# Gates below the smallest normal number set to zero, and an expert list of 96 blocks in place of 99

## The chip, the cores and the metric

The kernel runs on one core of a Trainium2 chip. The core has a matrix engine (TensorE, PE in the profile; its weight loads are PEld), three engines for elementwise work (VectorE or DVE, ScalarE or ACT, GpSimd or POOL), a queue engine (SyncE or SP), and 16 DMA engines that all queues share. The metric is the device time of one execution in microseconds; less is better.

## The reference

One layer of a diffusion backbone for 256 latent tokens with 256 context tokens: a modulated norm, one wide input projection, an mLSTM and a differential attention beside each other, their gated merge, and at the end a retrieval of single-neuron experts. Only the last part matters here:

```python
s = jnp.einsum('bthpd,hpnd->bthpn', q, sub_keys)
s1, i1 = lax.top_k(s[..., 0, :], P_TOPK)
s2, i2 = lax.top_k(s[..., 1, :], P_TOPK)
cand_s = (s1[..., :, None] + s2[..., None, :]).reshape(B, T, P_HEADS, P_TOPK * P_TOPK)
cand_i = (i1[..., :, None] * N_KEYS + i2[..., None, :]).reshape(B, T, P_HEADS, P_TOPK * P_TOPK)
top_s, pos = lax.top_k(cand_s, P_TOPK)
idx = jnp.take_along_axis(cand_i, pos, axis=-1)
g = jax.nn.softmax(top_s, axis=-1)
...
act = jax.nn.gelu(jnp.einsum('td,ted->te', hx, expert_u[ix]), approximate=False)
return jnp.einsum('te,ted->td', (gx * act).astype(h.dtype), expert_v[ix])
```

Each token has 8 heads, and each head picks 16 of 16,384 experts, with a softmax over the 16 scores as their gates. The scores lie far apart, so many gates are extremely small; the reference's arithmetic turns a result below the smallest normal number, 2^-126, into zero. An expert whose gate is zero for a token adds nothing to it.

## The kernel before

Everything is float32. Where full precision is wanted on TensorE, a tile is split into a rounded part `hi` (ScalarE) and the rest `lo` (VectorE), and three products of the parts are summed.

The 256 tokens form two tiles of 128, and each tile four groups of 32 tokens. The retrieval goes in these steps:

- **Choice and gates** (`retrieve`, run once for each tile). VectorE finds the 16 best of each head; L1176 to L1180 make the softmax: subtract the greatest, exponential on ScalarE, sum, reciprocal, product. The result `e`, 128 x 128, is transposed into `gT`.
- **Gate map** (`gate_map`). From the chosen indices and `gT`, one-hot matmuls build the full table of gates, experts by tokens, which goes to device memory; beside it `most` keeps, for each expert and each group of 32 tokens, the greatest gate.
- **Lists** (`lists`). A planner on VectorE, TensorE, ScalarE and GpSimd sorts the experts with a gate above zero (`use`, the test on `most`) into lists of blocks of 128 experts. There are eight lists for one group of 32 tokens (6 blocks each), one for each tile (7 each), one for both tiles (21), 16 for pairs of groups, one of each tile (1 block each): `CAPS`, 99 blocks in all. What finds no place in the lists before the last goes into the one for both tiles, and what finds none there is counted in `n_over`. Empty places of a block point at a fixed row with gates of zero: every block is gathered and multiplied whole, whatever it holds. At the end of the planner, one-hot tiles `N_BLOCKS` wide (L1408 to L1412, 32 rounds) and matmuls turn the places into the row numbers `idxV` and `idxG`.
- **First expert matrix.** Meanwhile TensorE multiplies all of `expert_u` with the tokens (`u_pair`), and the results, after the Gelu, go to the same table in device memory (`ag_dram`). The steps above are issued between these matmuls, a few at a time (`pump`, with the rate `pace`).
- **Second expert matrix.** For each block GpSimd issues two indirect gathers (L1501): 128 rows of `expert_v` (8 KB each) into `vraw`, and 128 rows of gates and activations into `ag`. VectorE multiplies gates and activations into weights. A block for one group of 32 needs, for each of its tiles, four matmuls of 128 x 32 weights (`v_groups`, four blocks beside each other on the array; each matmul has two records in the trace). A block of the lists for a tile or for both tiles (`v_block`) is split into two halves of `hi` and `lo` and needs 12 matmuls of 128 x 512 for each tile, which is 12 or 24. Two further blocks (`DENSE`) are taken whole.

The order of the second part is written out: 20 blocks of the first tile's groups (`SOON`) beside the end of `expert_u`, then `ITEMS`. These are two one-tile groups of four blocks, the two dense blocks, then a mixture made by `spread` (which puts the members of each list at equal distances): two more one-tile groups of four, four pair groups of four, the list for both tiles and the lists of the tiles; and three one-tile groups at the end. One letter an item (S a one-tile group of four, P a pair group of four, B a block for both tiles, T a block for one tile, D dense), `ITEMS` is

```
SSDDBTBTBPBTBSTBBTBPTBBTBTBBTPBTBBSTBTBPBTBTBSSS
```

which is 81 blocks. `fetch` (L1553) issues the gathers ahead of the work, in order; the gathers of GpSimd and the matmuls on these accumulators keep the order of the program. There are 12 buffers of rows, given out in pairs, two blocks a pair. `fetch` rounds block numbers to pairs:

```python
while staged[0] < end[0]:
    b = staged[0]
    if (b + 4 * (b >= L - 8)) // 2 * 2 - 11 >= FIRST_OF[n] or vex is None and b > 7:
        break
```

`L` is the number of blocks in `ITEMS`, `FIRST_OF[n]` the first block of item `n`. The last eight blocks, those of the last two items, are held back until four rows of other data (residual stream and norm weights, L1725 to L1729) have been given buffers. At the very end come, in program order: the third item from the end, which closes the first tile; the fetch for the item before the last; `residual` and `finish_tile` of the first tile; the item before the last; the fetch for the last item; the last item; the second tile's residual and output.

The loop at L1672 takes care of entries beyond the lists: it runs only if `n_over` is above zero, 126 turns, each with loads of 128 rows and their matmuls.

Of the kernel before, what the change touches and what calls it, by code (L numbers as in the profile page):

```python
# [26 lines left out]
OP = mybir.AluOpType  # L27
# [26 lines left out]

N_LIST = P - 2
EARLY = 104
CAPS = (6,) * 8 + (7, 7, 21) + (1,) * 16
BASE = tuple(sum(CAPS[:i]) for i in range(len(CAPS)))
BOTH, PAIR, DENSE = 10, 11, 27
TILES = [(g // 4,) for g in range(8)] + [(0,), (1,)] + [(0, 1)] * 17  # L60
# [6 lines left out]

N_BLOCKS = sum(CAPS)
NOWHERE = N_BLOCKS * P
# [3 lines left out]
def spread(*groups):  # L73
    return [x for _, _, x in sorted(((i + 0.5) / len(g), j, x) for j, g in enumerate(groups) for i, x in enumerate(g))]
# [4 lines left out]
SETS = [[[(4 * t + j, i) for j in range(4)] for i in range(6)] for t in range(2)]  # L79
SOON = SETS[0][:5]  # L80
PAIRS = [[(PAIR + 4 * d + g, 0) for g in range(4)] for d in range(4)]
ITEMS = SETS[1][:2] + [[(DENSE, i)] for i in range(N_LIST, P)] + spread(
    SETS[1][2:4], PAIRS, [[(BOTH, i)] for i in range(CAPS[BOTH])], [[(8 + n % 2, n // 2)] for n in range(14)]) + [
    SETS[0][5], SETS[1][4], SETS[1][5]]


def build(tc, a, dump=None):
    nc = tc.nc
# [6 lines left out]
    def turn(*args):  # L95
        tc.keep_in_program_order(nc.tensor.transpose(*args))
# [73 lines left out]
    def b3(t, n):  # L170
        return t.unsqueeze(2).to_broadcast([P, t.shape[1], n])
# [921 lines left out]
    for k in range(KT):  # L1093
# [4 lines left out]
                                       op0=OP.add, op1=OP.subtract)  # L1098
# [19 lines left out]
    def top16(src, vals, idx):  # L1118
        for r in range(2):
            v = vals[:, r * 8:(r + 1) * 8]  # L1120
            nc.vector.max(v, src)
            nc.vector.max_index(idx[:, r * 8:(r + 1) * 8], v, src)
            if r == 0:
                nc.vector.match_replace(src, v, src, NEG)
# [36 lines left out]
    def retrieve(t):  # L1161
        tif = tk.tile([P, 16, 16], F32, name="tif", tag="tif", bufs=1)
        nc.vector.tensor_copy(tif, ti[t])
        tv4 = tv[t].rearrange("p (h s) i -> p h s i", s=2)
        ti4 = tif.rearrange("p (h s) i -> p h s i", s=2)
        gv = tk.tile([P, HEADS, 16], F32, name="gv", tag="gv", bufs=1)
        gp = tk.tile([P, HEADS, 16], U32, name="gp", tag="gp", bufs=1)
        for h in range(HEADS):
            cs = tk.tile([P, 16, 16], F32, name="cs", tag="cs", bufs=2)
            nc.gpsimd.tensor_tensor(cs, b3(tv4[:, h, 0, :], 16),  # L1170
                                    tv4[:, h, 1, :].unsqueeze(1).to_broadcast([P, 16, 16]), op=OP.add)
            top16(cs.rearrange("p a b -> p (a b)"), gv[:, h, :], gp[:, h, :])
            yield
        e = tk.tile([P, HEADS, 16], F32, name="e", tag="e", bufs=1)
        z = tk.tile([P, HEADS], F32, name="zz", tag="zz", bufs=1)
        nc.vector.tensor_tensor(e, gv, gv[:, :, 0:1].to_broadcast([P, HEADS, 16]), op=OP.subtract)  # L1176
        nc.scalar.activation(e, e, AF.Exp)
        nc.vector.reduce_sum(z, e, axis=AX.X)
        nc.vector.reciprocal(z, z)
        nc.vector.tensor_tensor(e, e, b3(z, 16), op=OP.mult)  # L1180
        pos = tk.tile([P, 2, HEADS, 16], U32, name="pos", tag="pos", bufs=1)
        nc.vector.tensor_scalar(pos[:, 0], gp, 4, None, op0=OP.logical_shift_right)
        nc.vector.tensor_scalar(pos[:, 1], gp, 15, None, op0=OP.bitwise_and)
        posf = tk.tile([P, 2, HEADS, 16], F32, name="posf", tag="posf", bufs=1)
        nc.vector.tensor_copy(posf, pos)
        yield
        ii = []
        for s in range(2):
            r = tk.tile([P, HEADS, 16], F32, name="ix", tag=f"ix{s}", bufs=1)
            for h in range(HEADS):  # L1190
                if h % 4 == 0:
                    four = tk.tile([P, 4, 16, 16], F32, name="oh", tag="oh", bufs=1)
                oh = four[:, h % 4]
                nc.vector.tensor_tensor(oh, b3(posf[:, s, h, :], 16),
                                        iota[:, 0:16].unsqueeze(1).to_broadcast([P, 16, 16]), op=OP.is_equal)
                nc.gpsimd.tensor_tensor(oh, oh, ti4[:, h, s, :].unsqueeze(1).to_broadcast([P, 16, 16]),
                                        op=OP.mult)
                if h % 4 == 3:
                    yield
                    nc.vector.reduce_sum(r[:, h - 3:h + 1], four, axis=AX.X)  # L1200
                if h % 2:
                    yield
            ii.append(r)
        yield
        ps = psG.tile([P, 4, P], F32, name="g", tag="g")
        for i, src in enumerate((ii[0], ii[1], e)):
            turn(ps[:, i, :], src.rearrange("p h i -> p (h i)"), ident)
            nc.vector.tensor_copy(slots[i][:, t * P:(t + 1) * P], ps[:, i, :])
        yield
# [83 lines left out]
    def lists():  # L1293
# [46 lines left out]
        def fill(kind, size, bases):  # L1340
            n, w = kind.shape[1:]
            at = blocks_at[:, fills[0], 0:n]
            fills[0] += 1
            for c, base in enumerate(bases):
                nc.gpsimd.memset(at[:, c:c + 1], float(base * P - NOWHERE))
            pre, tot = (psG.tile([P, 4, P], F32, name="g", tag="g").rearrange("p a b -> p (a b)")[:, 0:n * w].rearrange(
                "p (c i) -> p c i", c=n) for _ in range(2))
            rank = ls.tile([P, 4, N_LIST], F32, name="rank", tag="rank", bufs=2)[:, 0:n, 0:w]
            pw = put[:, 0:n, 0:w]
            yield  # L1350
            yield
            mp_(pre, lhsT=from_on, rhs=kind, start=True, stop=True)
            mp_(tot, lhsT=one, rhs=kind, start=True, stop=True)
            yield
            for c in range(n):
                nc.vector.tensor_tensor_scan(rank[:, c], tot[:, c], zero[:, 0:w], 0.0, op0=OP.add, op1=OP.add)
            yield
            nc.vector.tensor_tensor(rank, rank, pre, op=OP.add)
            nc.vector.scalar_tensor_tensor(pw, rank, float(size * P), kind, op0=OP.is_lt, op1=OP.mult)
            nc.vector.reduce_sum(gone[:, 0:w], pw.rearrange("p c i -> p i c"), axis=AX.X)  # L1360
            nc.gpsimd.tensor_tensor(rank, rank, at.unsqueeze(2).to_broadcast([P, n, w]), op=OP.add)
            nc.gpsimd.tensor_tensor(rank, rank, pw, op=OP.mult)
            nc.gpsimd.tensor_tensor(places[:, 0:n, 0:w], places[:, 0:n, 0:w], rank, op=OP.add)
            yield
# [11 lines left out]
        for t in range(2):  # L1376
            four = single[:, 4 * t:4 * t + 4]
            for first, n, w in ((0, CAPS[0] - 1, EARLY), (CAPS[0] - 1, 1, N_LIST)):
                yield from fill(four[:, :, 0:w], n, [BASE[4 * t + c] + first for c in range(4)])
# [4 lines left out]
        nc.vector.tensor_tensor(k3[:, 0], k3[:, 0], k2[:, 1], op=OP.add)  # L1384
        yield from fill(k2, CAPS[8], [BASE[8 + c] for c in range(2)])
        nc.vector.tensor_tensor(k3[:, 0], k3[:, 0], gone, op=OP.subtract)
        yield
        yield from fill(k3, CAPS[BOTH], [BASE[BOTH]])
        over = ls.tile([P, N_LIST], F32, name="over")
# [60 lines left out]
    def plan():  # L1450
        nonlocal vst, gates
        yield from retrieve(0)
        for _ in weave(gate_map(0), retrieve(1)):
            yield
        tk.release()
        vst = tc.alloc_tile_pool(name="vst", bufs=1, side="right", reuse_waits="tile")
        yield from gate_map(1)
        while leaving:
            step(leaving)
            yield  # L1460
        pace[0] = 1.6
        yield from lists()
        gates = tc.alloc_tile_pool(name="ag", bufs=1, side="right", reuse_waits="tile")
        pace[0] = 1.3
        yield from soon()

    n = P - N_LIST + 1
# [346 lines left out]
```

## Time and profile before

| | |
|---|---|
| median of 3 runs | 2348.71 us (2344.53 to 2353.24) |
| the profiled execution | 2340.29 us, its span 2338.4 us |
| granted TensorE clock, mean | 0.981 |
| PE busy, 0 to 500 / to 1000 / to 1500 / to 2046 us | 476.6 / 489.3 / 475.5 / 513.3 us |
| PE busy, 2046 to 2338.4 us | 243.4 of 292.4 us |
| DMA share there, GB/s | 0.87, 344 |
| blocks gathered (rows of `expert_v`) | 99 |

The span is the time from the first to the last instruction of the profiled execution; its whole time is 1.9 us more. DMA share is the mean busy share of the 16 DMA engines. A group of instructions in the profile is given as line, engine, operation, out<-in by the program's names, count, busy time, mean duration of one, and the idle time of the engine before them with what ended it. Matmuls overlap their neighbours in the records, so a mean duration times a count is more than the time they take.

### The profile page before, as it was taken

How to read it: one execution, taken by the hardware profiler on the slowest of the kernel's cores; microseconds unless marked ns; L12 is line 12 of the kernel's file. 1: busy time of each engine (PE TensorE's matmuls, PEld its weight loads, DVE VectorE, ACT ScalarE, POOL GpSimd, SP SyncE). 2: the span in 40 equal slices, each digit the busy share in tenths (PEclk: the TensorE clock that was granted, in tenths of full speed). 3: DMA queues.
4: the chain of work that ended last, by engine and by line, in shares of the span. 5: the costliest groups of instructions: out<-in, count | busy, mean ns of one | idle time of the engine just before them, and what ended most of it. 6: DMA issues, size and time to landing. Idle time of an engine off the chain costs nothing.

```text
span 2338.4 us, 37404 instructions
## 1 busy us (share of the span) xinstructions
PE 2198.0 (94%) x14184; PEld 1880.2 (80%) x14184; DVE 1570.3 (67%) x2760; ACT 1057.4 (45%) x1723; POOL 935.0 (40%) x957
## 2 busy tenths in 40 slices
PE   6999999999999999998999999999999989999994
PEld 3669988999899999887987888888787776756661
DVE  3357973767876858746799766876799944454553
ACT  3232232244566744444444777995335433333431
POOL 2132210236534200002235755772456454566553
PEclk9999999999999999998999999999999999999997
DMA  9968964866456588755556457878665588899895
GB/s 380 351 212 304 332 228 134 316 206 192 144 150 203 169 280 283 272 191 176 172 174 209 160 183 222 229 213 238 197 194 172 184 330 321 330 414 387 333 395 190
DMA packets 235910, 570.98 MB, mean 244 GB/s; under 512 B 85154, under 2 KB 118739, under 8 KB 221264
## 3 DMA queue, kind: packets, MB, share of 16 engines
q1 hardware_dynamic: 153888, 339.34, 44.1%
q0 software_dynamic: 46992, 211.67, 25.1%
q10 hardware_dynamic: 34848, 17.57, 2.6%
q8 instruction: 111, 1.82, 0.3%
q14 instruction: 71, 0.58, 0.1%
HBM read 524.33 MB, written 38.93 MB: 241 GB/s over the span
## 4 chain that ended last, share of the span: by engine, by line
PE 69%; DVE 12%; DMA 6%; issue 5%; ACT 3%; POOL 2%; ACTq 0%; another core or an unknown queue 0%; SPq 0%; DVEq 0%; POOLq 0%
PE acc L289 24%; PE s L93 18%; PE acc L278 11%; PE v L93 9%; DVE lo L136 4%; DMA raw<-expert_u 3%; PE g L93 2%; ACT hi L133 2%; PE m L433 1%; DMA vraw<-expert_v,idxV 1%; PE m L278 1%; DMA raw<-w_mod 1%; DVE at L1409 1%; DVE act L1625 1%; PE m L382 1%
## 5 line engine op out<-in xcount | busy, mean ns | idle before, releaser
L133 ACT CAST hi<-raw 128x1024 fp32r<-128x1024 f32 x528 | 551.6, 1048 | 803.9 <-PE acc L289 256.7
L136 DVE TENSOR_TENSOR lo<-raw,hi 128x1024 fp32r<-128x1024 f32 x457 | 599.7, 1316 | 283.6 <-ACT hi L133 279.2
L93 PE MATMUL s<-h,hi 128*128 128x512 f32 x2048 | 743.3, 404 | 3.2 <-ACT hi L133 2.6
L93 PE MATMUL s<-h,lo 128*128 128x256 f32 x2048 | 581.3, 284 | 33.2 <-DVE lo L136 20.8
L93 PEld LDWEIGHTS s<-h,hi 128*128 128x128 f32 x2048 | 388.6, 190 | 96.0 <-ACT hi L133 6.3
L93 PEld LDWEIGHTS s<-h,lo 128*128 128x128 f32 x2048 | 390.7, 191 | 45.5 <-DVE lo L136 28.6
L289 PE MATMUL acc<-hL,hi 128*128 128x256 f32 x2048 | 421.7, 286 | 0.0
L289 PEld LDWEIGHTS acc<-hL,hi 128*128 128x128 f32 x2048 | 342.5, 193 | 1.5
L289 PE MATMUL acc<-hL,lo 128*128 128x256 f32 x1024 | 292.3, 286 | 4.6 <-DVE lo L136 4.6
L136 POOL TENSOR_TENSOR lo<-raw,hi 128x1024 fp32r<-128x1024 f32 x71 | 176.9, 2492 | 254.3 <-ACT hi L133 248.6
L289 PEld LDWEIGHTS acc<-hL,lo 128*128 128x128 f32 x1024 | 197.5, 193 | 6.2 <-DVE lo L136 5.5
L117 POOL DMA_DIRECT2D raw<-w_mod x128 | 68.2, 533 | 300.2 <-DVE raw L522 278.7
L522 DVE SCALAR_TENSOR_TENSOR raw<-raw,cr 128x1024 f32<-128x1024 f32 x128 | 154.7, 1219 | 32.4 <-DMA raw<-w_mod 17.6
L1241 POOL TENSOR_SCALAR o<-iota,i1T,gT 128x128 f32<-128x128 f32 x128 | 138.9, 1092 | 93.1 <-PE g L93 49.3
L1517 DVE TENSOR_TENSOR lo<-vraw,hi 128x1024 fp32r<-128x1024 f32 x74 | 90.3, 1228 | 100.5 <-ACT hi L1515 76.1
L1501 POOL DMA_INDIRECT vraw<-expert_v,idxV x99 | 106.6, 1077 | 97.7 <-PE v L93 38.1
L289 PE MATMUL acc<-hC,hi 128*128 128x256 f32 x512 | 134.0, 283 | 0.0
L1515 ACT CAST hi<-vraw 128x1024 fp32r<-128x1024 f32 x74 | 77.1, 1049 | 115.0 <-PE v L93 56.1
L93 PE MATMUL v<-hi,l 128*128 128x512 f32 x448 | 123.5, 394 | 4.0 <-issue 3.1
L1625 DVE TENSOR_REDUCE act<-s 128x256 f32<-128x512 f32 x126 | 86.2, 684 | 53.6 <-PE s L93 48.2
L1501 POOL DMA_INDIRECT ag<-ag_dram,idxG x99 | 106.3, 1074 | 33.6 <-issue 27.3
L93 PE MATMUL v<-vraw,w 128*32 128x512 f32 x640 | 90.2, 642 | 28.5 <-DVE w L1536 12.9
(427 smaller groups left out, 3859.9 us busy)
## 6 DMA issues: line engine op xcount, KB each, us to landing
raw<-expert_u SPq DMA_DIRECT2D x256, 512.0 KB
raw<-w_in SPq DMA_DIRECT2D x176, 512.0 KB
raw<-w_mod POOLq DMA_DIRECT2D x128, 512.0 KB
raw<-w_mod SPq DMA_DIRECT2D x64, 512.0 KB
raw<-w_out SPq DMA_DIRECT2D x32, 512.0 KB
raw<-w_pq SPq DMA_DIRECT2D x32, 512.0 KB
ag_dram<-gates SPq DMA_DIRECT2D x32, 512.0 KB
ag_dram<-act ACTq DMA_DIRECT2D x126, 128.0 KB
```

The lines of the kernel that those rows point to most:

```text
L93: tc.keep_in_program_order(mm(*args, **kw))
L117: d = queue.dma_start(r, src)
L133: nc.scalar.copy(h, r)
L136: (nc.vector if shared[0] else nc.gpsimd).tensor_tensor(l, r, h.bitcast(F32), op=OP.subtract)
L278: mm(acc[ti], lhsT=lhs(sa, ti, 2 * kp + k2), rhs=hl[sb][:, k2 * 512:(k2 + 1) * 512], start=first and k2 == 0 and i == 0, stop=last and k2 ...
L289: mm(acc[c][:, g * T:(g + 1) * T], lhsT=hl[sb][:, k2 * 512 + c * P:k2 * 512 + (c + 1) * P], rhs=rhs(sa, g, k), start=first and k2 == 0 and ...
L522: product = nc.vector.scalar_tensor_tensor(r, r, 1.0, cr, op0=OP.mult, op1=OP.mult, accum_out=part[:, h, i:i + 1])
L1241: (nc.gpsimd if i % 2 else nc.vector).tensor_scalar(o2[:, i, 0:width], iota[:, 0:width], cols[:, i:i + 1], factor[:, i:i + 1], op0=OP.is_e ...
L1501: tc.keep_in_program_order(nc.gpsimd.indirect_dma_start(out=out, out_offset=None, in_=src, in_offset=bass.IndirectOffsetOnAxis(ap=idx[:, b ...
L1515: nc.scalar.copy(h, raw)
L1517: nc.vector.tensor_tensor(l, raw, h.bitcast(F32), op=OP.subtract)
L1625: nc.vector.reduce_sum(act[:, e], ps.rearrange("p s t -> p t s"), axis=AX.X)
```

## The change

Three things. The tiles' lists get 8 blocks each in place of 7, and the list for both tiles 16 in place of 21; so 96 blocks in place of 99, and in `ITEMS` 78 in place of 81. `spread` places 16 blocks of each kind. And in `retrieve` one more VectorE instruction, behind the product of the softmax, multiplies each gate by whether it is at least 2^-126.

```diff
-CAPS = (6,) * 8 + (7, 7, 21) + (1,) * 16
+CAPS = (6,) * 8 + (8, 8, 16) + (1,) * 16
...
-    SETS[1][2:4], PAIRS, [[(BOTH, i)] for i in range(CAPS[BOTH])], [[(8 + n % 2, n // 2)] for n in range(14)]) + [
+    SETS[1][2:4], PAIRS, [[(BOTH, i)] for i in range(CAPS[BOTH])], [[(8 + n % 2, n // 2)] for n in range(16)]) + [
     SETS[0][5], SETS[1][4], SETS[1][5]]
...
         nc.vector.tensor_tensor(e, e, b3(z, 16), op=OP.mult)
+        nc.vector.scalar_tensor_tensor(e, e, 2.0 ** -126, e, op0=OP.is_ge, op1=OP.mult)
         pos = tk.tile([P, 2, HEADS, 16], U32, name="pos", tag="pos", bufs=1)
```

In the letters above, `ITEMS` becomes

```
SSDDBTBTPBTBTSBTBTPBTBTBTBTPBTBTSBTBTPBTBTSSS
```

## The prediction

> **What bounds the kernel now.** I read the page first, then the windows of the last 300 us, then the groups of instructions and the waits in them. The page says that TensorE has work nearly everywhere, so a cut in matmuls can pay; it doesn't say where.
>
> ```profile
> span 2338.4 us, 37404 instructions
> PE 2198.0 (94%) x14184; PEld 1880.2 (80%) x14184; DVE 1570.3 (67%) x2760; ACT 1057.4 (45%) x1723; POOL 935.0 (40%) x957
> ```
>
> The lists are used only after about 2046 us, when the first expert matrix is done and the rows of the second are gathered block by block. I cut that stage where its behaviour changes (columns: window, its length, busy us and instructions of PE, PEld, DVE, ACT, POOL, then granted clock, DMA share, GB/s):
>
> ```profile
> 2046.00:2128.00 82.00, 72.45 (x374) 46.37 (x373) 37.79 (x75) 27.34 (x41) 55.22 (x52) 0.98 1.02 413
> 2128.00:2290.00 162.00, 155.40 (x780) 106.37 (x779) 84.27 (x165) 62.45 (x92) 90.18 (x84) 0.99 0.92 363
> 2290.00:2318.00 28.00, 10.06 (x50) 2.15 (x46) 7.21 (x18) 3.50 (x9) 15.58 (x14) 0.65 0.65 243
> ```
>
> Three regimes. Up to 2128 the DMA engines are full (share 1.02 at 413 GB/s, which I take as full) and PE idles 9.6 us. From 2128 to 2290 PE is busy for 155.4 of 162 us, and the DMA engines have 162 x (1 - 0.92/1.02) = 15.9 us to spare. After 2290 neither is busy: a chain of small steps. What PE does and waits for in the second regime, and the work of the first two together:
>
> ```profile
> PE v L93 <- issue: 4.9, 4, 3.1
> PE v L93 <- DVE lo L1517: 1.1, 2, 0.5
> PE v L93 <- ACT hi L1515: 0.7, 1, 0.7
> ```
>
> ```profile
> L93 PE MATMUL v<-hi,l 128*128 128x512 f32 x448 | 123.5, 394 | 4.0 <-issue 3.1 <-ACT hi L1515 0.7
> L1501 POOL DMA_INDIRECT ag<-ag_dram,idxG x68 | 73.7, 1084 | 20.8 <-issue 20.4 <-DMA vraw<-expert_v,idxV 0.3
> L1501 POOL DMA_INDIRECT vraw<-expert_v,idxV x68 | 72.5, 1066 | 71.5 <-PE v L93 26.7 <-issue 16.0 <-DVE w L1536 13.5
> L93 PE MATMUL v<-lo,l 128*128 128x512 f32 x224 | 70.5, 396 | 1.6 <-DVE lo L1517 1.1 <-issue 0.5
> L93 PE MATMUL v<-vraw,w 128*32 128x512 f32 x416 | 57.0, 613 | 10.5 <-issue 4.0 <-DMA vraw<-expert_v,idxV 3.6 <-DVE act_tail L1625 2.1
> ```
>
> The 448 + 224 = 672 split matmuls are exactly the lists in question: 14 one-tile blocks x 12 and 21 two-tile blocks x 24. The gathers' own largest wait is for PE (26.7 us): rows are read no faster than PE frees their buffers.
>
> **The change part by part.** (1) Matmuls. After it there are 16 x 12 + 16 x 24 = 576, so 96 fewer. A matmul's mean of 394 ns overlaps its neighbours, so I take the pace from an unbroken stretch of the timeline of PE:
>
> ```profile
> 2193.78 1.07 PE L93 MATMUL v<-hi,l 128*128 128x512 f32 x4
> 2194.69 0.61 PE L93 MATMUL v<-lo,l 128*128 128x512 f32 x2
> ...
> 2203.31 1.07 PE L93 MATMUL v<-hi,l 128*128 128x512 f32 x4
> 2204.21 0.61 PE L93 MATMUL v<-lo,l 128*128 128x512 f32 x2
> 2204.67 0.61 PE L93 MATMUL v<-hi,l 128*128 128x512 f32 x2
> 2205.21 7.07 PE L93 MATMUL v<-vraw,w 128*32 128x512 f32 x64
> ```
>
> From 2193.78 to 2203.31 lie 7 rounds of 6, 42 matmuls in 9.53 us: 0.227 us each, so 96 are worth 21.8 us of PE.
>
> Not all of it shows. The order spreads lists and groups; between the start and the one-tile group of four that ends the first regime it puts five two-tile and three one-tile blocks, and will put four and four. That removes 12 matmuls (2.7 us) there, but that group waits for its rows:
>
> ```profile
> 2118.69 3.30 PE L93 MATMUL v<-vraw,w 128*32 128x512 f32 x19
> 2122.40 0.63 PE L93 MATMUL v<-vraw,w 128*32 128x512 f32 x2 [0.41 <-issue]
> 2124.51 1.32 PE L93 MATMUL v<-vraw,w 128*32 128x512 f32 x2 [1.49 <-issue]
> 2126.66 0.60 PE L93 MATMUL v<-vraw,w 128*32 128x512 f32 x1 [0.83 <-issue]
> 2128.10 1.10 PE L93 MATMUL v<-vraw,w 128*32 128x512 f32 x8 [0.84 <-issue]
> ```
>
> The 26 blocks through this group stay 26, and one of them reads a gate row half as wide (131 KB less, 0.3 us at 413 GB/s). So 2128 stays 2128, and the 2.7 us become waiting. In the 162 us after it, two-tile blocks go from 16 to 12 and one-tile blocks from 11 to 12: 84 matmuls fewer, 19.1 us.
>
> (2) Gathers. A block reads 128 rows of 8 KB (1.05 MB) and gate rows of 0.26 MB (two tiles) or 0.13 MB (one). In the 162 us that is 4 x 1.31 - 1.18 = 4.06 MB less, 9.8 us at 413 GB/s, and three pairs of POOL issues fewer (about 2.1 us each by the rows above; POOL was busy 90 of 162 us and hides them).
>
> So the stretch is bounded thus. By PE alone: 162 - 19.1 = 143. By DMA alone, with no pause: 162 - 15.9 - 9.8 = 136; with all of today's pauses: 152. PE's 143 is above DMA's 136, but the margin is only 7 us and rows come in bursts, so I add 2 us of new row waits: **145, a gain of 17**, with 9.8 and 19.1 as its ends.
>
> (3) The order at the end. The fetch rule (L1553) rounds block numbers down to even ones. With 81 blocks in the list the last one, 80, gives 84 - 11 = 73, which isn't below 73, the first block of the item before the last; it is fetched only with the last item, behind that item's predecessor. With 78 blocks, block 77 gives 80 - 11 = 69, below 70, and goes out with the three before it. Likewise the item before the last gets all four of its blocks a step earlier (70 to 73), where block 76 now comes late. What that costs now, from the timeline:
>
> ```profile
> 2294.10 1.25 POOL L1501 DMA_INDIRECT vraw<-expert_v,idxV  x1 [0.15 <-issue]
> ...
> 2301.93 0.95 POOL L1501 DMA_INDIRECT vraw<-expert_v,idxV  x1 [0.30 <-issue]
> ...
> 2306.48 6.25 PE L93 MATMUL v<-vraw,w 128*32 128x512 f32 x32 [8.62 <-DVE w L1536]
> 2306.85 1.06 POOL L1501 DMA_INDIRECT ag<-ag_dram,idxG  x1 [0.18 <-issue]
> 2312.14 0.96 POOL L1501 DMA_INDIRECT vraw<-expert_v,idxV  x1 [4.23 <-PE v L93]
> 2317.78 5.70 PE L93 MATMUL v<-vraw,w 128*32 128x512 f32 x26 [5.05 <-DMA vraw<-expert_v,idxV]
> ```
>
> Four row gathers leave from 2294.10 to 2301.93; the fifth waits for PE until 2312.14, and the last item starts at 2317.78, 5.6 us after it. Without the fifth the last item waits for the gather of 2301.93. By the same 5.6 us its rows are there at 2307.6; four gathers at once and the outputs of the first tile make it about 2310. **Gain 7.5**, with ends 0 (POOL or the buffers put the fourth gather as late as the fifth is now) and 10.2.
>
> (4) Narrower lists and the added line. The one-hot rows of the planner go from 99 to 96 columns, in a stretch where VectorE is full:
>
> ```profile
> 1750.00:1860.00 110.00, 104.06 (x635) 86.74 (x634) 107.97 (x118) 54.90 (x73) 63.23 (x47) 1.00 0.53 172
> L1409 DVE TENSOR_TENSOR at<-hl,iota 128x396 bf16<-128x396 f32 (+1 forms) x32 | 29.1, 916 | 0.0
> 1201.56 0.59 DVE L1176 TENSOR_TENSOR e<-gv 128x128 f32<-128x128 f32 x1
> 1215.18 2.08 DVE L1180 TENSOR_TENSOR e<-e,zz 128x128 f32<-128x128 f32 x1
> 1291.43 0.29 DVE L1180 TENSOR_TENSOR e<-e,zz 128x128 f32<-128x128 f32 x1
> ```
>
> 3/99 of 29.1 us is 0.9 us, gained at most. The added line runs twice, on 128x128; the same shape took 0.29, 0.59 and 2.08 us, so 0.6 to 4.2 us in all on an engine that other work presses there (below nothing isn't possible: it only adds). I take 0.3 each, the undisturbed row: **+0.6**. It adds no wait: it stands between two instructions of one engine.
>
> **Sum:** -17 - 7.5 - 0.9 + 0.6 = -24.8 us. The profiled execution ran 2340.3 us (span 2338.4, 1.9 around it) and would run 2315.5. The median of the timed runs shown is 2348.7, 8.4 us above it; from there the forecast is **2324 us**.
>
> **The rivals.** *A: the DMA engines take over.* If pauses between gathers stay as they are, the stretch gains only its bytes, 9.8 us. For it: share 0.92 already; PE's idle up to 2128 is all row waits. Against: the gathers' largest wait is for PE. With half of the end's gain, -9.8 - 3.8 - 0.3 gives about 2335. Chance 0.25. [...] I hold against it that PE shows only 6.7 us of waits there. [...]
>
> ```profile
> 2180.00:2190.00 10.00, 6.37 (x24) 4.12 (x23) 4.57 (x10) 4.33 (x7) 5.37 (x5) 0.95 1.02 417
> 2190.00:2200.00 10.00, 10.00 (x41) 8.19 (x40) 6.20 (x12) 3.82 (x6) 4.59 (x4) 0.88 0.83 319
> ```
>
> After 3.6 us of idle PE the granted clock fell to 0.88. [...]
>
> *B: the time saved turns into waiting whole.* The stretch and the end give nothing beyond a few us, because a later gather sets both; the added line costs up to 4.2 us. About 2345. Chance 0.08.
>
> *C: the lists no longer hold the entries.* One entry over 16 blocks of 128 starts the loop at L1672: 126 turns, each with eight loads into a single buffer. By the 5.05 us that PE waited for one landing, 40 us a turn, 5 ms in all: about 7400 us. Against it: with the reference's gates on its inputs I count 7.6 and 7.9 blocks for the tiles and 13.1 for both, so all fit. The loop's lines have no instruction in the trace, though with gates below the smallest normal number kept I count 23.3 blocks for the 21 there were; so the chip drops them already, and the new line changes few entries or none. *That it doesn't do what it says* thus costs nothing here: block counts are fixed in the program. Chance 0.03.
>
> **How the numbers follow.** The forecast has 0.64, A 0.25, B 0.08, C 0.03. A measurement tells 0.5% (11.7 us, below 2337) from no change. Faster: the forecast and 0.19 of A, 0.83. Same: the rest of A and nearly all of B, 0.13. Slower: C and 0.01 of B, 0.04. The range goes from all bounds on the good side (-19.1 - 10.2 - 0.9 and 6 us of vanished waits, 2312) to rival A without the end's gain (2341).
>
> **What would show it.** The windows from 2128: 17 us shorter, DMA share at 0.97 or more, PE's waits for rows up by a few us. If share stays 0.92 and the gain is 10, it is A. The first four-block group still ends at about 2128. In the last chain no row gather waits for PE after the residual of the first tile, and the last item starts about 10 us earlier after the first tile's last matmul. The added line shows two instructions below 2.1 us. A different order of instructions before 2046 that moves that point by over 5 us would upset the sum.

## The result, and the profile after

| | kernel before | changed kernel | ratio, 95% interval |
|---|---|---|---|
| first comparison (median of 6 and 6) | 2347.56 us | 2310.42 us | 0.9841, 0.9815 to 0.9866 |
| later comparison (17 and 4) | 2325.92 us | 2301.69 us | 0.9898, 0.9884 to 0.9913 |
| profiled executions of the first | 2340.29 us | 2309.84 us | |

The change is faster by 37 us in the first comparison, by 24 us in the later one. The forecast was 2324 us with a range from 2312; 2310.4 lies 1.6 us below it. One of the six executions of the kernel before took 2707 us; without this slow one its median is 2346.4. The two profiled executions are 30.5 us apart, the medians of the first comparison 37.1.

The busy time of each engine from the changed kernel's page:

```profile
PE 2175.0 (94%) x14088; PEld 1861.5 (81%) x14088; DVE 1556.3 (67%) x2740; ACT 1048.8 (45%) x1709; POOL 928.1 (40%) x951
```

96 matmuls and 3 pairs of gathers are gone, as the lists say. For the comparison I cut each run at two points that exist in all of them: the start of the last reduction of the first expert matrix (tile `act_tail`, "Gelu" below) and the start of the first residual product (`yf`, when the first tile's last matmuls are coming out). Windows between these points and to the end of the span, kernel before:

```profile
2051.50:2288.10 236.60, 221.85 (x1108) 149.61 (x1112) 120.01 (x237) 89.79 (x133) 142.41 (x132) 0.99 0.95 380
2288.10:2338.40 50.30, 17.43 (x88) 3.79 (x80) 17.40 (x32) 7.73 (x19) 19.05 (x17) 0.67 0.43 162
```

The changed kernel (columns as in the prediction: length; PE, PEld, DVE, ACT, POOL; clock, DMA share, GB/s):

```profile
2050.90:2267.50 216.60, 202.32 (x1012) 131.22 (x1016) 109.59 (x216) 82.32 (x119) 136.63 (x128) 0.98 0.98 394
2267.50:2307.70 40.20, 12.65 (x88) 3.90 (x80) 18.72 (x31) 7.63 (x19) 17.30 (x16) 0.71 0.57 218
```

Nearly the whole gain lies behind the Gelu: 20.0 us in the gathers and 10.1 us at the end, against 0.6 us ahead of them. The added line, by source line of the changed kernel (min/median/max in ns, first and last start):

```profile
L1181 DVE SCALAR_TENSOR_TENSOR e<-e x2: 267/276/284, 1219.3 to 1290.4; 128x128 f32<-128x128 f32 x2
```

Two instructions of 0.28 us, as costed. What PE waited for between the two points (in total, how often, longest, in us), first in the kernel before, then in the changed one:

```profile
PE v L93 <- issue: 7.6, 7, 3.1
PE v L93 <- DMA vraw<-expert_v,idxV: 3.6, 1, 3.6
```

```profile
PE v L93 <- issue: 10.1, 7, 5.4
PE v L93 <- DMA vraw<-expert_v,idxV: 0.8, 1, 0.8
```

In both, PE's largest wait is "issue": for nothing that the profile shows. It was already so in the group of four before 2128 us whose gaps the prediction took for a wait for rows. Those gaps lie between single matmuls in the second half of the group, and its first four matmuls already need all four rows. The later runs of the table below have no such wait on PE in this stretch, and that is where the first comparison parts from the others.

One thing limits what these two profiles can tell of a wait: they hold no landing time for any transfer, while all the later ones do. Their line for the row gathers, first in the kernel before, then in a later profile of it (the last number is the time from issue to landing):

```profile
vraw<-expert_v,idxV POOLq DMA_INDIRECT x99
```

```profile
vraw<-expert_v,idxV POOLq DMA_INDIRECT x99, 11.1
```

A wait that a landing ended may therefore stand in the first two profiles as one without a cause; that is an inference, which no run shows.

### The profile page after: what moved, and what is told of

It is laid out like the page before. It is cut to its first block, busy times and chain, and to the rows that moved or that the text cites. A ratio compares the mean times of both kernels' runs of the same rounds, so it can differ in the third digit from the quotient of the medians.

```text
span 2307.7 us, 37149 instructions
## 1 busy us (share of the span) xinstructions
PE 2175.0 (94%) x14088; PEld 1861.5 (81%) x14088; DVE 1556.3 (67%) x2740; ACT 1048.8 (45%) x1709; POOL 928.1 (40%) x951
## 4 chain that ended last, share of the span: by engine, by line
PE 67%; DVE 13%; DMA 7%; issue 6%; ACT 3%; POOL 3%; ACTq 0%; DVEq 0%; another core or an unknown queue 0%; SPq 0%; POOLq 0%
PE acc L289 23%; PE s L93 18%; PE acc L278 11%; PE v L93 7%; DVE lo L136 4%; DMA raw<-expert_u 3%; PE g L93 2%; ACT hi L133 2%; PE m L433 1%; DMA ag<-ag_dram,idxG 1%; DMA raw<-w_mod 1%; PE m L278 1%; POOL lo L136 1%; DMA vraw<-expert_v,idxV 1%; DVE act L1626 1%
## 5 line engine op out<-in xcount | busy, mean ns | idle before, releaser
L1518 DVE TENSOR_TENSOR lo<-vraw,hi 128x1024 fp32r<-128x1024 f32 x68 | 83.0, 1227 | 95.4 <-ACT hi L1516 54.8
L1502 POOL DMA_INDIRECT vraw<-expert_v,idxV x96 | 100.8, 1050 | 90.4 <-PE v L93 25.4
L1516 ACT CAST hi<-vraw 128x1024 fp32r<-128x1024 f32 x68 | 70.8, 1048 | 108.7 <-PE v L93 59.1
L93 PE MATMUL v<-hi,l 128*128 128x512 f32 x384 | 108.9, 401 | 8.3 <-issue 6.5
L278 PE MATMUL acc<-hi,hL 128*128 128x512 f32 x320 | 110.0, 402 | 0.5 <-ACT hi L133 0.5
```

The costliest lines, as they stand in the source:

```text
L93: tc.keep_in_program_order(mm(*args, **kw))
L278: mm(acc[ti], lhsT=lhs(sa, ti, 2 * kp + k2), rhs=hl[sb][:, k2 * 512:(k2 + 1) * 512], start=first and k2 == 0 and i == 0, stop=last and k2 ...
L1502: tc.keep_in_program_order(nc.gpsimd.indirect_dma_start(out=out, out_offset=None, in_=src, in_offset=bass.IndirectOffsetOnAxis(ap=idx[:, b ...
L1516: nc.scalar.copy(h, raw)
L1518: nc.vector.tensor_tensor(l, raw, h.bitcast(F32), op=OP.subtract)
```

## The experiments

All ratios are to the kernel before in the same comparison. "Lists" gives the blocks of the lists for the first tile, the second tile and both tiles. "Gelu at", "Gelu to yf" and "yf to end" are in us and from each run's one profile, so a difference of a few us in them is not by itself a finding; the ratios are over several executions. Two more runs, e2 and e12, took thousands of us and are told below.

| run | lists | ratio, interval | Gelu at | Gelu to yf | yf to end |
|---|---|---|---|---|---|
| before (first profile) | 7, 7, 21 | | 2051.5 | 236.6 | 50.3 |
| changed (first profile) | 8, 8, 16 | 0.9841 | 2050.9 | 216.6 | 40.2 |
| e7_before_again | 7, 7, 21 | 1.0003 (0.9991 to 1.0015) | 2057.5 | 219.4 | 49.9 |
| e8_changed_again | 8, 8, 16 | 0.9898 (0.9884 to 0.9913) | 2053.4 | 201.9 | 44.3 |
| e1_line | 7, 7, 21 | 1.0013 (0.9998 to 1.0028) | 2053.6 | 218.9 | 49.7 |
| e3_after_late | 8, 8, 16 | 0.9923 (0.9904 to 0.9943) | 2059.3 | 203.5 | 44.3 |
| e4_before_early | 7, 7, 21 | 1.0001 (0.9983 to 1.002) | 2053.1 | 220.1 | 48.9 |
| e5_fourteen | 8, 8, 14 | 0.9863 (0.9849 to 0.9877) | 2051.5 | 199.2 | 41.1 |
| e6_two_passes | 8, 8, 16 | 0.9908 (0.9894 to 0.9923) | 2057.6 | 206.9 | 41.4 |
| e9_pairs | 7, 7, 21 | 1.0015 (0.9999 to 1.0031) | 2054.6 | 219.3 | 51.5 |
| e10_both | 7, 7, 21 | 1.0011 (0.9995 to 1.0026) | 2052.4 | 219.4 | 49.9 |
| e13_before_two_passes | 7, 7, 21 | 0.9993 (0.9979 to 1.0007) | 2056.8 | 215.6 | 50.3 |
| e14_aligned | 7, 7, 21 | 0.997 (0.9955 to 0.9984) | 2059.8 | 219.3 | 43.5 |
| e16_twentytwo | 7, 7, 22 | 0.9996 (0.9981 to 1.001) | 2056.1 | 224.3 | 42.0 |
| e17_twenty | 7, 7, 20 | 0.9949 (0.9927 to 0.997) | 2053.2 | 215.9 | 42.9 |

**The line and the lists apart.**

```diff
+        nc.vector.scalar_tensor_tensor(e, e, 2.0 ** -126, e, op0=OP.is_ge, op1=OP.mult)
```

> The kernel before with the added line alone, lists of 7, 7 and 21 blocks. Theory (the line costs its two instructions and nothing else): +0.6 us, ratio 1.000. Rival (the line changes what the lists hold or shifts the order of other work, and part of the 37 us is its): faster by 5 us or more. Rival (it stretches the chain on VectorE as the dear product row did): +4.2 us.

1.0013: the line costs nothing that can be told. It also empties more places in the lists, and the time doesn't show that either.

e2 is the changed kernel without that line.

> The changed kernel without the added line (gates below the smallest normal number are not set to zero by an instruction). Theory (all of the gain is the list sizes'): within 2 us of the changed kernel, 30 to 37 us below the kernel before. Rival (without the line the lists overflow and the loop of 126 turns runs): thousands of us more. Rival (the line is needed for part of the gain): 5 us or more above the changed kernel.

It took 6865 us. The rival held that the lists overflow without the line. In its waits:

```profile
POOL ag L1501 <- DVE w L1539: 4559.4, 1, 4559.4
```

The gathers stand still for 4559 us while the loop runs its 126 turns, 36.2 us each. So without the line some gates below the smallest normal number are still above zero, and the smaller lists need the line. How many are kept, e12 narrows down (changed kernel without the line, 18 blocks for both tiles, one execution):

```diff
-CAPS = (6,) * 8 + (8, 8, 16) + (1,) * 16
+CAPS = (6,) * 8 + (8, 8, 18) + (1,) * 16
```

> The changed kernel without the added line and with 18 blocks for both tiles in place of 16. It tells how many entries the line takes out of the lists. Theory (the chip keeps about half of the gates below the smallest normal number; all of them would need 21 blocks with 8 for each tile): the loop runs, thousands of us more. Rival (only a few entries were over 16 blocks): no loop, about 10 us more than the changed kernel.

6856 us: the loop ran. By my count with 8 blocks for each tile the list for both needs 13.1 blocks without these gates and 21.3 with all; with 7, 14.6 and 23.3. The counts are made from the reference and its inputs, not measured. More than 18 of the first pair and at most 21 of the second (the kernel before runs no loop) put the share of these entries that is kept between about 0.6 and 0.74, an estimate that takes the need for blocks to grow evenly with that share.

**The same two kernels again.**

> The changed kernel once more, beside new runs of the kernel before. In its first profile the kernel before had engines that waited for nothing that the profile shows during the gathers (PE 7.6 us, ScalarE over 50 us); the runs of it with one edit each had none of that on PE and took 15 to 20 us less. Theory (those waits made the first gain larger than the lists are worth): the gain is 16 us in the gathers and 5 to 10 at the end, 21 to 26 us, ratio 0.989 to 0.991. Rival (37 us are the lists'): ratio 0.984.

> The kernel before, unchanged, for a second profile. Theory (waits without a visible cause differ from execution to execution, or from chip to chip): from the last Gelu to the first tile's last matmul 219 us as in the runs with one edit, in place of 237; PE waits for nothing unseen. Rival (the two edits removed them): 237 us again and PE with 7 us of such waits.

The ratio was 0.9898, 24.2 us, and the kernel before fell from 2347.6 to 2325.9 us with nothing changed in it. The later comparisons, on chips 0, 3 and 7, agree: its medians there lie from 2323.8 to 2325.9. Which chip the first comparison ran on is not on record, so a difference between chips was not ruled out. The new profile of the kernel before, the same two windows:

```profile
2057.50:2276.90 219.40, 212.40 (x1116) 147.20 (x1120) 119.99 (x237) 90.07 (x133) 141.56 (x133) 0.98 1.01 410
2276.90:2326.80 49.90, 16.23 (x88) 3.51 (x80) 17.49 (x32) 7.73 (x19) 19.04 (x17) 0.72 0.50 188
```

The changed kernel beside it:

```profile
2053.40:2255.30 201.90, 195.97 (x1026) 129.84 (x1025) 108.94 (x215) 82.10 (x119) 135.94 (x127) 0.98 1.02 413
2255.30:2299.60 44.30, 13.48 (x85) 4.27 (x77) 18.94 (x32) 7.62 (x19) 17.73 (x16) 0.69 0.64 254
```

The gathers' stretch of the kernel before is 17 us shorter than in its first profile, and the DMA share in it is 1.01 and not 0.95. PE has one kind of wait left there, for rows (6.9 us). ScalarE shows the difference best. Its waits from 2064 to 2250 us in the first profile of the kernel before:

```profile
ACT hi L1515 <- issue: 32.8, 12, 8.5
ACT hi L1515 <- remote: 16.2, 5, 4.7
```

and in the second:

```profile
ACT hi L1515 <- issue: 9.2, 7, 1.5
```

So the theory held in part: waits without a visible cause, up to 8.5 us long, lay over the first comparison, and they came and went with the comparison, not with an edit. That the kernel before had more of them is not shown: the changed kernel's first profile has 26.1 and 14.5 us in the same two rows, and on PE 10.1 us beside 7.6. From the first profiles to the later ones the gathers' stretch fell by 17.2 us in the kernel before and by 14.7 in the changed one. What ended these waits stays open, the more so as the first two profiles hold no landings.

With 413 GB/s as full (the DMA share was 1.02 at that rate in e8), GB/s times length gives the bytes, and the rest of the time is idle DMA. Kernel before: 219.4 x 0.410 + 49.9 x 0.188 = 99.3 MB, 240.5 us of transfer, 28.8 us idle. Changed: 94.6 MB, 229.1 us, 17.1 us idle. The gain of 23.1 us behind the Gelu is thus 11.4 us of bytes and 11.7 us of idle DMA time, and 10 of the 11.7 lie in the last window. (The other 4.1 us of these two profiles lie ahead of the Gelu, whose time went from 2050.9 to 2059.8 over all runs without a pattern.)

**Matmuls or bytes.** Both kernels without the third product, which leaves out the low part of the weights times the high part of the rows in the list blocks and dense blocks:

```diff
-        for sa, sb in PASS:
+        for sa, sb in PASS[:2]:
             for c in range(2):
                 mp_(out_acc[t][hf_ * 2 + c], lhsT=ins[sa], rhs=hl[sb][:, c * 512:(c + 1) * 512],
```

> The changed kernel without the third product (low part of the weights with the high part of the rows) in the blocks of the tiles' lists and the two dense blocks: 208 matmuls fewer, the same gathers. Theory (PE sets the pace): 208 x 0.227 = 47 us less than the changed kernel, less what the DMA engines then hold back. Rival (DMA is at its limit already): 0 to 8 us less, DMA share at 1.02 throughout.

> The kernel before without the third product (low part of the weights with the high part of the rows) in the blocks of the tiles' lists and the two dense blocks: 240 matmuls fewer, the same gathers. Theory (before the change the gathers' stretch was held by matmuls and by row reading about equally, so that fewer matmuls alone let the DMA engines hold it): 5 to 12 us less, ratio 0.995 to 0.998. Rival (matmuls alone set it): 54 us less, 0.977. Rival (row reading alone set it): no change, and the change's gain there was its bytes, 10 us.

The rivals held, against both theories: 208 matmuls fewer gave the changed kernel nothing (0.9908 beside 0.9898), 240 fewer gave the kernel before nothing (0.9993). The gathers' window of e13:

```profile
2056.80:2272.40 215.60, 184.18 (x882) 105.47 (x882) 120.58 (x236) 88.63 (x133) 144.52 (x132) 0.93 1.02 413
```

PE is busy 28 us less than in e7, at a granted clock of 0.93 and not 0.98. The DMA engines are as full as before, and the stretch is 4 us shorter. So in the later comparisons it is the row reading that holds this stretch: the 6.6 MB that the changed kernel reads less in it (219.4 x 0.410 - 201.9 x 0.413) are 15.9 us at 413 GB/s, of the 17.5 us that it is shorter. The other side, bytes, with two blocks fewer in the changed kernel:

```diff
-CAPS = (6,) * 8 + (8, 8, 16) + (1,) * 16
+CAPS = (6,) * 8 + (8, 8, 14) + (1,) * 16
```

> The changed kernel with 14 blocks for both tiles in place of 16 (94 in all); by my count 13.1 blocks are used. Theory (PE sets the pace of the gathers): 48 matmuls fewer, 10.9 us less than the changed kernel. Rival (DMA sets it): 2.62 MB less at 413 GB/s, 6.3 us. Rival (the chip keeps more gates than I count): the loop runs, thousands of us more.

8.1 us less than the changed kernel by the medians (2293.58), between the two sums and nearer to that of the bytes, without ruling the other out; from the Gelu on, its profile is 5.9 us shorter. It is the fastest of these kernels, but 14 blocks hold the entries of these inputs only: for two other draws of them I count 14.7 and 14.5.

**The end.** The prediction's reason was the fetch rule. One digit moves the last blocks an item later or earlier.

```diff
-            if (b + 4 * (b >= L - 8)) // 2 * 2 - 11 >= FIRST_OF[n] or vex is None and b > 7:
+            if (b + 5 * (b >= L - 8)) // 2 * 2 - 11 >= FIRST_OF[n] or vex is None and b > 7:
```

> The changed kernel with 5 in place of 4 in the fetch rule for the last eight blocks: block 73 goes out one item later and block 77 only with the last item, as blocks 76 and 80 did before. Same lists, same matmuls. Theory (the end's gain is the even number of blocks): the part from the first tile's last matmul to the end goes back from 40 to about 50 us, the time rises by 10 us, ratio to the kernel before 0.988. Rival (the end got shorter for another reason, such as rows in other buffers): no change from the changed kernel, 0.984.

> The kernel before with 3 in place of 4 in the fetch rule for the last eight blocks: blocks 76 and 80 go out one item earlier each. Same lists, same matmuls. Theory (late fetch of the last block costs the end 10 us): the end shrinks from 50 to about 40 us, 10 us faster, ratio 0.996. Rival (with 81 blocks the buffer of block 80 comes free only after the item before it, whatever the rule): less than 2 us.

The theory failed twice. The changed kernel with the late fetch kept its end of 44.3 us (its ratio is a little above that of e8, with overlapping intervals); the kernel before with the early one (3 in that place) kept 48.9 and 1.0001. My second theory was the buffers of the four rows of other data:

```diff
+    one_row()
     fw, g2, *x1 = [one_row() for _ in range(4)]
```

> The kernel before with one row buffer left unused ahead of the four rows of other data, so that they fill two pairs of buffers and not parts of three, as in the changed kernel. Lists and fetch rule as before. Theory (an odd number of blocks pins three of six pairs at the end, so block 80 waits for the item before it): the row gather of block 80 no longer waits for TensorE, the part from the first tile's last matmul to the end shrinks from 50 to 44 us, ratio 0.9975. Rival (the shorter end comes from something else): 1.000.

> The kernel before with the unused row buffer and with 3 in place of 4 in the fetch rule, so that the last block is also fetched an item earlier. Theory (both are needed: the early fetch alone gave nothing because the buffer was not free): the end at 44 us or less, ratio 0.996 to 0.9975. Rival (the end depends on how much of the row reading is still to be done when it begins): about 50 us, 1.000.

It failed too: 1.0015, and with the early fetch 1.0011. GpSimd's queue in e7 shows what was left to explain (of the five row gathers after 2276.9, when the first tile is done, the last; the other four start from 2282.88 to 2290.69):

```profile
2300.26 0.95 POOL L1501 DMA_INDIRECT vraw<-expert_v,idxV  x1 [3.59 <-PE v L93]
```

Five row gathers start only after the first tile's last item, four in the changed kernel. Buffers are given in pairs; blocks 69 to 72, the item that closes the first tile, begin at an odd number and lie across three pairs. The pair of 68 and 69 is then free a whole item later, and the fifth gather comes last. In the changed kernel that item is blocks 66 to 69, two whole pairs. The two edits with the unused buffer, e9 and e10, did not shorten this queue: they leave the buffer unused behind that item, and six row gathers come after the first tile's end. Three runs tell the item from the rest. The first has the early fetch of e10 and the unused buffer ahead of the item and not behind it,

```diff
-            if (b + 4 * (b >= L - 8)) // 2 * 2 - 11 >= FIRST_OF[n] or vex is None and b > 7:
+            if (b + 3 * (b >= L - 8)) // 2 * 2 - 11 >= FIRST_OF[n] or vex is None and b > 7:
                 break
+            if b == L - 12:
+                one_row()
             ins = stage_gates(*BLOCKS_OF[b])
```

> The kernel before with one row buffer left unused ahead of block 69, so that the item that closes the first tile (blocks 69 to 72) fills two pairs of buffers and not parts of three, and with 3 in place of 4 in the fetch rule. Lists as before. Theory (that item's alignment sets how many gathers wait for its end): four row gathers and not five start after the first tile's last matmul, the end falls from 50 to 44 us, ratio 0.9975. Rival (the end is longer for its bytes or for the order of GpSimd's work): 50 us, 1.000.

the second has a block more and so an even number (22 in place of 21), and the third a block fewer (20, with the added line):

> The kernel before with 22 blocks for both tiles: 82 blocks in the order, an even number, 1.31 MB more to read. Theory (even alignment saves up to 10 us of idle DMA time at the end, 1.31 MB cost 3.2 us): 2 to 7 us faster than the kernel before, 0.997 to 0.999. Rival (only the bytes count): 3.2 us slower, 1.0014. Rival (the matmuls count): 5.4 us slower, 1.0023.

> The kernel before with the added line and 20 blocks for both tiles: 80 blocks in the order, an even number, 1.31 MB less to read. Theory: bytes and alignment together, 3.2 and 5 to 10 us: 0.994 to 0.9965. Rival (only the bytes count): 0.9986.

e14 and e17 came out as expected, e16 just outside. In e14 (yf at 2279.1) four row gathers are left, the last of them 13.9 us behind yf, not 23.4:

```profile
2292.97 0.94 POOL L1501 DMA_INDIRECT vraw<-expert_v,idxV  x1 [0.30 <-issue]
```

Its end is 43.5 us and its ratio 0.997 (0.9955 to 0.9984), with not one instruction of arithmetic or byte less; e10, which differs from it only in the place of the unused buffer, has 49.9 us and 1.0011 (0.9995 to 1.0026). e16 reads 1.31 MB more than the kernel before and is not slower (0.9996, just above the upper end of what I gave); e17 reads 1.31 MB less and gains 12 us (0.9949), more than the 3.2 us of the bytes.

What goes with the end is how many row gathers come after the first tile's end, not when the last of them goes out. With four it took 40.2 to 44.3 us, with five 48.9 to 50.3, with six 49.9 and 51.5. The time of the last gather doesn't order the runs: in e3 it goes out 18.7 us behind yf and the end is 44.3 us, in e10 18.8 us behind and the end is 49.9.

## Why the prediction was right or wrong

**Direction and the sum.** Faster was right, and -24.8 us was the working's sum: the later comparison measured -24.2, the first -37.1. The range failed by 1.6 us in the first. That the sum met the later comparison is luck in good part: the runs contradict the reasons given for both of its large terms, as told below.

**The step that failed it: the base.** "From there the forecast is 2324 us" put the sum on the median of three runs, 8.4 us above the profiled execution, as if that offset would stay. It didn't: the changed kernel's profile lies within 0.6 us of its median. That is 7.8 us of the miss; the other 5.7 us are those by which the two profiles differ more than the sum, 3.0 of them in the gathers and 2.6 at the end. From the profiled execution, 2340.3 us, the same bounds would have given a range from 2304, with the result inside. Why the kernel before took 2338.9 us or more in every execution of the first comparison, and 2325.9 in the median of the later one, no run shows. That its time held something not its own could be suspected from the rows that I quoted: 4.9 us of "issue" on PE, and the gaps within one group of four, which I read as waits for rows (of PE's 9.6 us up to 2128, only 3.6 are put down to rows). The upper end of the range, 2341, doesn't come out of its terms either: 2348.7 - 9.8 + 0.6 is 2339.5.

**"PE's 143 is above DMA's 136".** The limit was wrong, and the size was near by luck. In the later profiles PE and the DMA engines are both busy nearly throughout (in e7 PE for 212 of 219 us, at a DMA share of 1.01), and it is the reading of rows that holds: 240 matmuls fewer gained nothing in the kernel before (e13, 0.9993). The stretch shrank by 17.5 us where I said 17, but about 6.6 MB less were read in it: the lists' own 4.2 MB and some 2 MB that moved behind the first tile's end. Rival A (bytes alone, 9.8 us) had the right limit and too few bytes. (The 3.6 us of idle PE that the prediction has ahead of the granted clock of 0.88 are two waits, of 3.1 and 0.5 us; what lowered the clock no run shows.)

**"2128 stays 2128".** In the first profiles it moved: that group of four ended at 2119.2 in the changed kernel, 10 us earlier. Its gaps in the kernel before were no wait for rows, since matmuls that need all four rows had run ahead of them; what they were stays open.

**The end, 7.5 us.** Measured 10.1 in the first profiles and 5.6 in the later ones. The place was right, an odd number of blocks; the step from the fetch rule to it was wrong, for a late or an early fetch alone changed the end by 1 us or less (e3, e4). How the closing item lies in its pairs of buffers sets it: with that put right in the kernel before, e14 gained 7 us (0.997).

**The added line.** Its cost was right, 0.55 us for 0.6. "The chip drops them already, and the new line changes few entries or none" was wrong: without it the lists overflow. I took "no loop in the trace" for "all dropped" where it only says that 21 blocks were enough. Rival C's price was right in kind (36.2 us a turn for 40), and it is the price of the lists without the line.

**The narrower lists, 0.9 us.** They can't be told apart from the scatter of the Gelu's time, some 9 us over all profiles.

## What to carry to other kernels

Where an engine and the DMA queues are both full, take work off one of them in an experiment before a gain is put down to it: PE was busy for 212 of 219 us here, and 240 of its matmuls (54 us at 0.227 us each) could go without any gain (e13, 0.9993). A change in the number of work items can shift how they lie in paired buffers, and that alone was worth 0.3 per cent here (e14); look at which gathers wait for which item at the end. And a wait that the profile puts down to nothing need not be the kernel's own (7.6 us on PE in the first profile of the kernel before, none in the second): look whether a second profile has it, and whether the profile holds landing times at all, before carrying it into a forecast.

## What the runs showed of the hardware

With row gathers of 128 rows of 8 KB, and their gate rows beside them, the core read 401 to 413 GB/s over the 199 to 224 us of the gathers' stretch in the later profiles (401 in e16, 413 in e8); with the added line in the kernel before, which by my count points more places of the blocks at one row, the time was the same (1.0013 in e1 and 1.0003 in e7, at 407 and 410 GB/s). The softmax on ScalarE and VectorE leaves gates below 2^-126 that are not zero (e2, without the added line, ran the loop and took 6865 us), and a comparison on VectorE, two instructions of 0.28 us, takes them out (the changed kernel with it runs no loop, 2310.4 us). And one program took 2347.6 us in one comparison and 2325.9 in another; in the two profiles the gathers' stretch differs by 17.2 us, with a DMA share of 0.95 in the longer and 1.01 in the shorter, and the cause is not shown.
